# A bidirectional attention and mLSTM layer: a hand-ordered opening with four output tiles, modulation dot products moved later, pauses ahead of TensorE's in-order steps

## The chip, the cores and the metric

The kernel runs on one core of one Trainium2 chip. The metric is the device time of one execution in microseconds (us). Its engines work side by side, each through its own instructions in order: TensorE (PE in the profile, PEld for its weight loads), VectorE (DVE), ScalarE (ACT), GpSimd (POOL), and SyncE (SP), which here only issues DMAs.

## The reference, cut to what matters

One layer over 1024 tokens of width 1024, all in float32:

```python
cond = silu(c)
mod = cond @ w_ada + b_ada                      # 6 x 1024 values: 48 columns of 128
sh1, sc1, g1, sh2, sc2, g2 = split(mod, 6)
h = rms_norm(x, norm_mix_g) * (1 + sc1) + sh1
q_a, k_a, v_a, qk_m, v_m, o_m, gates = split(h @ w_in)
y_attn = axial_gqa_attention(q_a, k_a, v_a)     # 8 heads of 64, 2 key/value heads
y_mem = bidirectional_mlstm(qk_m, v_m, o_m, gates)   # 4 heads of 128, conv of 5 taps before
x = x + g1 * (concat(y_attn, y_mem) @ w_out)
h = rms_norm(x, norm_ffn_g) * (1 + sc2) + sh2
x = x + g2 * ((silu(h @ w_gate) * (h @ w_up)) @ w_down)
return rms_norm(x, final_norm_g)
```

## The kernel before

**Matmuls.** Activations lie transposed: 8 tiles of 128 channels x 1024 tokens. Each float32 product is made of three matmuls on a high and a low part (fp32r): `hi*hi`, `hi*lo`, `lo*hi` (`mm3`, L297 to L300). So each operand is split into a high part by ScalarE (`whi`, `hh`) and a low part by GpSimd or VectorE (`wlo`, `hl`). One output tile of 128 columns takes 2 token halves x 8 channel tiles x 3 = 48 matmuls of 512 columns.

**Order.** The program is one straight list for each engine. It is not written by hand: a planner (`Clock`, `Engine`, `Stream`) keeps a model time, runs chains of steps (`ck.chain`) when their modelled inputs are ready, and lets fill units (`un`) of the list `IN` run on TensorE whenever the main streams would wait by the model. What a step issues on an engine stands in that engine's order for good; if the real time differs from the model's, the engine waits there and all behind it waits too.

**Stages.** (1) The opening (L487 to L611): x is loaded, squares are summed by VectorE and GpSimd into `ssx`, a matmul with `ones` adds over the channels (`ms`, L553), VectorE and ScalarE make 1/rms; warm-up matmuls fill TensorE (`WARM0` 9 and `WARM` 6 calls, L551 and L559). The modulation is a dot product over the condition for each of the 48 columns: a 128 x 1024 tile `ada` of weights, multiplied and summed by one VectorE instruction (`ada_load`, L96 by way of the helper). For each channel tile k two of them (scale and shift) are needed before `h_steps(k)` can make `x*rstd` (VectorE), the scale and shift (ScalarE), `hh` (ScalarE) and `hl` (GpSimd; VectorE for k = 0). TensorE sums three output tiles (the attention's k, v and first q) over k. (2) The rest of the input projection up to the attention, by the list `IN`: the token chunk `t0` with the gate columns, then q tiles, then `f` tiles with their five-tap convolutions; beside it the rotary steps (`rope_steps`) of k and q and the chain of the gates (`gate_steps`), each of which puts small matmuls into TensorE's order (`squares` L641 to L651, `columns` L908, `spread` L922). Meanwhile `ada_late` loads and sums further modulation columns in halves of 512, one for each model microsecond. (3) The attention with fill units. (4) The mLSTM with the last token chunks as fill, then, behind a loop that waits for the last of the 64 late half dot products, the output projection (list `MIX`) as fill. (5) The FFN with its products made by a seven-product scheme; nothing of it is touched.

**Names.** `POOLED` sends the dot product of column 0 to GpSimd and ScalarE. `PP["cond"]` is SiLU(c) on all 128 partitions, loaded 128 times by one DMA of 512 KB. `k2` are the high and low parts of the rotated keys; both must be there before the attention starts. `ready()` ends stage 2: it asks for the last q tile's rotation and the gates.

Of the kernel before, what the change touches and what calls it, by code (L numbers as in the profile page):

```python
# [11 lines left out]
F32 = mybir.dt.float32  # L12
# [3 lines left out]
OP = mybir.AluOpType  # L16
# [24 lines left out]
WARM = 6  # L41
WARM0 = 9
POOLED = (0,)
# [4 lines left out]
IN = ([("t", 0), ("q", 1), ("q", 2), ("q", 3), ("f", 0), ("f", 4), ("f", 1), ("f", 5), ("t", 2), ("f", 2), ("f", 6),  # L48
# [192 lines left out]
def layer_kernel(ctx, tc, xT, c, w_ada, vecs, cons, rope, w_f, w_t0, w_t, w_o, w_gu, w_d, out):  # L241
# [9 lines left out]
    both = const.tile([P, 2], F32, name="both")  # L251
# [6 lines left out]
    nc.scalar.dma_start(con, cons)  # L258
# [30 lines left out]
    nc.vector.tensor_copy(selr, C("sel"))  # L289
    identb = mid.tile([P, P], BF16, name="identb")  # L290
    nc.vector.tensor_copy(identb, ident)
    maskb = mid.tile([P, 2, 2, P], BF16, name="maskb")
    for i in range(2):
        nc.vector.tensor_copy(maskb[:, 0, i], C("maskf"))
        nc.vector.tensor_copy(maskb[:, 1, i], C("maskb"))
# [55 lines left out]
    with tc.manual_schedule():  # L351
# [10 lines left out]
        bp = PP["ada"] = big_open(5)  # L362

# [8 lines left out]
        va = kvp.tile([P, NJ, 2, P], F32R, name="va")  # L372
        k2 = [[kvp.tile([P, S], F32R, name=f"k2{i}{g}") for i in range(2)] for g in range(2)]
# [37 lines left out]
        specs = conv_w(0) + conv_w(1) + conv_w(2)  # L411
# [74 lines left out]
        psum_open("ps0", {n: ("ps0", 8) for n in ("acc", "acct", "ms", "tr", "T")}, 8)  # L486

        def small():
            return stp.tile([P, HALF], F32, tag="sq", name="sq", bufs=4)

        load_cond(bp)
        ck.table = "silu"
        x_t = [stp.tile([P, S], F32, tag="x", name=f"x{k}", bufs=KT) for k in range(KT)]
        msp = [psum_any([P, HALF], "ms") for _ in range(NH)]
        ssx = [stp.tile([P, HALF], F32, tag="ssx", name="ssx", bufs=2) for _ in range(NH)]
        sq_ok = {}
        for k in range(KT):
            def sum_up(k=k):

                for n in range(NH):  # L500
                    sq = ssx[n] if k == 0 else small()
                    act.activation(sq, x_t[k][:, halves(n)], AF.Square)
                    if k:
                        (gps if n and k < 6 else dve).tensor_add(ssx[n], ssx[n], sq)

            sq_ok[k] = ck.chain(dma(x_t[k], xT[k]), sum_up)
        ada_at = {}
        rstd_done = Flag()

        def ada_load(j):  # L510
            t = bp.tile([P, D], F32, tag="big", name="ada")
# [7 lines left out]

        for j in (8, 0):  # L520
            ada_load(j)
        load_piece()
        load_piece()
        ck.need(sq_ok[4])
        load_piece()
# [1561 lines left out]
```

## Time and profile before

| | us |
|---|---|
| median of 3 runs (1403.0 to 1405.35) | 1405.2 |
| the profiled execution | 1407.29 |
| its span, first to last instruction | 1405.5 |
| TensorE busy | 1300.5 (93%) |
| VectorE busy | 1065.1 (76%) |
| ScalarE busy | 662.9 (47%) |
| GpSimd busy | 679.0 (48%) |
| mean granted TensorE clock | 0.972 |

Busy time counts an instruction from start to end; matmuls overlap, so that one of 0.40 us is followed by the next after less. A granted clock of 1.00 is 2.4 GHz and 0.50 is 1.2 GHz. A line of L96 is the helper through which the planner issues all ScalarE, VectorE and GpSimd work: such rows are told apart by their tiles, written out<-in. "[7.23 <-ACT hh L96]" at the end of a row is the idle time of the engine before it and what ended it.

### The profile page before, as it was taken

To read this page: it belongs to the slowest core of one execution; us is meant where nothing else is said; L and a number is where in the kernel's file an instruction comes from. 1 tells how busy PE (TensorE), PEld (TensorE's weight loads), DVE (VectorE), ACT (ScalarE), POOL (GpSimd) and SP (SyncE) were. 2 spreads that over 40 slices of the span, in tenths; PEclk is the share of its full clock that TensorE was granted. 3 is DMA by queue.
4 is the path that set the end of the run, shared out by engine and by line. 5 is a ranking of instruction groups with operands and counts; after the bars stand their busy time and mean duration, and the time that the engine had idled before them with its cause. 6 is when DMAs were issued, how large, how long until landed. Compare 5 with 4: busy or idle time off the path is not lost.

```text
span 1405.5 us, 19481 instructions
## 1 busy us (share of the span) xinstructions
PE 1300.5 (93%) x6594; PEld 1072.1 (76%) x6602; DVE 1065.1 (76%) x1600; ACT 662.9 (47%) x1194; POOL 679.0 (48%) x555
## 2 busy tenths in 40 slices
PE   5789798999999989899996999999999999979997
PEld 2578577889878979777774888888888887757887
DVE  7947979986788848768589886666666654798866
ACT  5454316677666655454476333332332334344463
POOL 5555554545344336577421355454544545545542
PEclk9899989999999999999998999999999999989999
DMA  7446462322122146553552333322332259723324
GB/s 287 165 128 203 135 172 80 108 77 65 38 65 70 35 140 211 188 203 115 196 187 75 113 120 105 107 104 100 110 113 90 71 175 327 275 81 102 93 65 154
DMA packets 103172, 184.40 MB, mean 131 GB/s; under 512 B 11296, under 2 KB 32672, under 8 KB 103072
## 3 DMA queue, kind: packets, MB, share of 16 engines
q1 hardware_dynamic: 89968, 161.06, 36.0%
q10 hardware_dynamic: 13104, 22.10, 4.2%
q8 instruction: 52, 0.85, 0.2%
q14 instruction: 48, 0.39, 0.1%
HBM read 136.19 MB, written 43.25 MB: 128 GB/s over the span
## 4 chain that ended last, share of the span: by engine, by line
PE 61%; DVE 20%; DMA 6%; issue 5%; ACT 3%; POOL 3%; SPq 1%; DVEq 0%; ACTq 0%; POOLq 0%
PE acc L299 15%; PE acc L298 15%; PE acc L300 15%; DVE x L96 3%; PE av L1029 3%; DVE ada L96 3%; DVE sst L96 2%; PE T L1010 2%; DVE PT L96 2%; PE S L978 2%; DVE y L96 1%; PE acct L298 1%; PE acct L300 1%; PE acct L299 1%; DVE wd L96 1%
## 5 line engine op out<-in xcount | busy, mean ns | idle before, releaser
L96 POOL TENSOR_TENSOR wlo<-wst,whi 128x512 fp32r<-128x512 f32 (+2 forms) x196 | 279.5, 1432 | 285.0 <-ACT whi L96 272.9
L96 ACT ACTIVATE whi<-wst 128x512 fp32r<-128x512 f32 (+2 forms) x219 | 131.0, 605 | 125.1 <-POOL wlo L96 25.3
L96 POOL TENSOR_SCALAR P<-P,sst 128x1024 f32<-128x1024 f32 x64 | 88.9, 1392 | 141.1 <-DVE sst L96 106.4
L299 PE MATMUL acc<-x,whi 128*128 128x512 f32 x352 | 140.7, 400 | 5.9 <-DVE x L96 5.9
L96 POOL TENSOR_TENSOR wlo<-wr,whi 128x512 fp32r<-128x512 f32 x56 | 76.9, 1374 | 77.4 <-ACT whi L96 73.9
L298 PE MATMUL acc<-hh,whi 128*128 128x512 f32 x224 | 97.5, 435 | 14.1 <-ACT hh L96 11.8
L298 PE MATMUL acc<-whi,wch 128*128 128x512 f32 x244 | 97.2, 398 | 6.3 <-ACT wch L96 6.3
L96 ACT ACTIVATE P<-S,sst,colq 128x1024 f32<-128x1024 f32 x64 | 77.3, 1207 | 52.4 <-DVE sst L96 47.9
L299 PE MATMUL acc<-hl,whi 128*128 128x512 f32 x224 | 92.4, 412 | 8.2 <-POOL hl L96 4.5
L300 PE MATMUL acc<-whi,wcl 128*128 128x512 f32 x244 | 97.2, 398 | 2.9 <-DVE wcl L96 2.8
L299 PE MATMUL acc<-wlo,wch 128*128 128x512 f32 x244 | 97.0, 398 | 0.6 <-POOL wlo L96 0.5
L96 DVE SCALAR_TENSOR_TENSOR ada<-ada,cond 128x512 f32<-128x512 f32 (+1 forms) x79 | 80.2, 1023 | 18.3 <-DMA ada<-in_w_ada_dram 12.7
L300 PE MATMUL acc<-hh,wlo 128*128 128x512 f32 x224 | 91.5, 409 | 0.0
L96 DVE TENSOR_TENSOR sg<-acc,sg 128x512 f32<-128x512 f32 x67 | 45.4, 687 | 58.8 <-PE acc L300 58.5
L96 ACT ACTIVATE PT<-T 128x512 fp32r<-128x512 f32 x128 | 71.4, 597 | 37.7 <-PE T L1010 36.9
L96 ACT ACTIVATE whi<-wr 128x512 fp32r<-128x512 f32 x60 | 37.9, 632 | 108.1 <-DVE wr L96 50.3
L96 DVE TENSOR_TENSOR PT<-T,PT 128x512 fp32r<-128x512 f32 x128 | 82.8, 681 | 7.2 <-ACT PT L96 7.1
L96 POOL TENSOR_TENSOR wlo<-s,whi 128x512 fp32r<-128x512 f32 x40 | 53.8, 1347 | 70.7 <-ACT whi L96 70.7
L299 PEld LDWEIGHTS acc<-x,whi 128*128 128x128 f32 x352 | 67.0, 190 | 22.3 <-DVE x L96 7.3
L298 PE MATMUL acct<-whi,hh 128*128 128x256 f32 (+1 forms) x256 | 79.4, 310 | 2.5 <-ACT xp L96 1.2
L96 DVE TENSOR_TENSOR wcl<-wd,wch 128x512 fp32r<-128x512 f32 x50 | 48.0, 972 | 42.1 <-ACT wch L96 26.9
L1010 PE MATMUL T<-con,P 128*128 128x128 f32 x512 | 70.3, 275 | 10.2 <-DVE PT L96 7.4
(459 smaller groups left out, 3802.5 us busy)
## 6 DMA issues: line engine op xcount, KB each, us to landing
wr<-in_w_gu_dram SPq DMA_DIRECT2D x66, 256.0 KB, 2.8
ada<-in_w_ada_dram SPq DMA_DIRECT2D x64, 256.0 KB, 3.3
wd<-in_w_d_dram SPq DMA_DIRECT2D x22, 512.0 KB, 7.0
wst<-in_w_gu_dram SPq DMA_DIRECT2D x34, 256.0 KB, 3.1
wst<-act_d SPq DMA_DIRECT2D x33, 256.0 KB, 4.1
ada<-in_w_ada_dram SPq DMA_DIRECT2D x16, 512.0 KB, 5.5
wst<-in_w_o_dram SPq DMA_DIRECT2D x32, 256.0 KB, 4.3
act_d<-sg ACTq DMA_DIRECT2D x31, 256.0 KB, 2.0
```

Of the source, the lines that this page charges most:

```text
L96: return fn(*args, **kw)
L298: nc.tensor.matmul(acc, w[0], x[0], start=first, stop=False)
L299: nc.tensor.matmul(acc, w[0], x[1], start=False, stop=False)
L300: nc.tensor.matmul(acc, w[1], x[0], start=False, stop=last)
L978: nc.tensor.matmul(sp[:, halves(n)], qs[:, j * P:(j + 1) * P], k2[g][m][:, halves(n)], start=m == 0, stop=m == 1)
L1010: nc.tensor.transpose(tp[:, k], Pt[q][:, (4 * b + k) * P:(4 * b + k + 1) * P], ident)
L1029: nc.tensor.matmul(av, va[:, k, h // 4], PT[it][m][:, k], start=(k, m) == (0, 0), stop=(k, m) == (NJ - 1, 1))
```

## The change

- **Opening by hand, four tiles.** The opening's instructions are written out for each engine in a fixed order instead of by the planner (`ve, ac, gp` are the bare engines). TensorE sums four tiles (k, v, first and second q) instead of three, so 24 matmuls for each k, and the list `IN` loses `("q", 1)`. The condition is loaded as one row of 4 KB, SiLU is taken on it, and two matmuls with `ones` spread it over the partitions. The squares are added on VectorE alone (x tiles in pairs), and each pair is summed at once by two matmuls into the same bank. The warm-up is 3 + 3 + 5 calls instead of 9 + 6. `hl` is made by VectorE for every k; `hh` is made by one ScalarE step from x (the separate scaled copy of x is gone); GpSimd makes only the low parts of weights. No dot product goes to GpSimd.
- **Second q tile.** `rope_steps(1)`, which takes its sums out of their banks, is chained behind both halves of `k2`.
- **Dot products later.** No late half dot product is issued in stage 2; the attention takes 32 (before: up to 48 by its end); the other 32 are issued beside the whole mLSTM, first in the old pool, then in another four-buffer ring once the first tiles of the attention's output are split. The loop that waits for the last of them stands behind the mLSTM instead of ahead of the output projection.
- **Pauses.** `later(dt)` adds model time: 2.5 us ahead of `squares`, 6.0 us ahead of the `columns` transposes, 5.0 us ahead of `spread`.

```diff
-WARM = 6
-WARM0 = 9
-POOLED = (0,)
+WARM = 5
+WARM0 = 3
+NT0 = 4
-IN = ([("t", 0), ("q", 1), ("q", 2), ("q", 3), ("f", 0), ("f", 4), ("f", 1), ("f", 5), ("t", 2), ("f", 2), ("f", 6),
+IN = ([("t", 0), ("q", 2), ("q", 3), ("f", 0), ("f", 4), ("f", 1), ("f", 5), ("t", 2), ("f", 2), ("f", 6),
...
+        gp.memset(crow, 0.0)
+        nc.sync.dma_start(crow[0:1], c)
+        for k in range(KT):
+            nc.sync.dma_start(x_t[k], xT[k])
...
+        ac.activation(both[:, 2:3], eps, AF.Silu)
+        ac.activation(crow[0:1], crow[0:1], AF.Silu)
+        ac.activation(both[:, 2:3], eps, AF.Abs_reciprocal_sqrt)
+        for n in range(NH):
+            nc.tensor.matmul(cb[n], ones, crow[:, halves(n)], start=True, stop=True)
...
+            if k % 2:
+                for n in range(NH):
+                    nc.tensor.matmul(msp[n], ones, a[:, halves(n)], start=k == 1, stop=k == KT - 1)
+                if k < KT - 1:
+                    nc.tensor.matmul(acc0[0][0], ones, crow[:, 0:HALF], start=True, stop=True)
...
+        dot(8)
+        gain(0)
+        root_v(0)
+        root_y(0)
+        ac.activation(msp[0], ry[0], AF.Square)
+        first_hi(0, 0)
+        first_lo(0, 0, gp)
+        dot(0)
+        shift(0)
+        root_y(1)
+        root_end(0)
+        first_hi(0, 1)
+        first_lo(0, 1, gp)
+        xr(0, 0)
+        h_hi_of(0, 0)
+        root_v(1)
...
+        def prepare(k):
+            if k + 1 < KT:
+                if k > 1:
+                    ada_load(9 + k)
+                ada_load(k + 1)
+            dot(8 + k)
+            gain(k)
+            dot(k)
+            shift(k)
             for n in range(NH):
+                xr(k, n)
+                h_hi_of(k, n)
+            for n in range(NH):
+                h_lo_of(k, n)
+            if k < 5:
+                first_hi(1, k - 1)
+                first_lo(1, k - 1, gp)
...
-            ck.chain(0.0, lambda: evac(0), lambda: evac(1), swap, squares)
+            ck.chain(0.0, lambda: evac(0), lambda: evac(1), swap, later(2.5), squares)
...
-                     lambda: exps(0), lambda: exps(1), state, lambda: exps(2),
+                     lambda: exps(0), lambda: exps(1), state, lambda: exps(2), later(6.0),
...
+                     lambda: dve.tensor_scalar(cols[:, :, 1], cols[:, :, 1], QK, None, op0=OP.mult), decay, later(5.0), spread,
...
+        rope_steps(4, [(a, Flag()) for a in acc0[0]])
         v_steps([(a, Flag()) for a in acc0[1]])
-        rope_steps(4, [(a, Flag()) for a in acc0[0]])
         ck.at(2.5, lambda: rope_steps(0, [(a, Flag()) for a in acc0[2]]))
+        ck.chain(0.0, *k2_ok, lambda: rope_steps(1, [(a, Flag()) for a in acc0[3]]))
...
         def ready():
-            if ck.t > t_ada[0]:
-                ada_late()
-                t_ada[0] = ck.t + 1.0
...
-        while len(adas) < 48:
+        while len(adas) < 32:
...
-        while not summed:
-            ck.need(*adas[-2:])
-            ada_late(64)
-        ck.tick = None
+        ck.need(*adas[-2:])
+        PP["ada_new"] = lambda: mp.tile([P, HALF], F32, tag="yat", name="ada", bufs=4)
+        ck.tick = lambda: (0, 0) in Y and all(y[2].done for y in Y[0, 0]) and ada_late(64)
...
         ck.streams([un], stop=lambda: not open_sum[0])
+        while not summed:
+            ck.need(*adas[-2:])
+            ada_late(64)
+        ck.tick = None
```

## Rows read from the trace of the kernel before

**Rows 1.** The table by stage: for each stretch (us from the span's start) its length, then busy us and instructions of each engine, granted clock, busy share of the DMA engines, GB/s. The stretches are the opening, the rest of the projection ahead of the attention, the attention, the mLSTM with the last token chunks, and the mLSTM with the output projection.

```profile
0.00:89.00 89.00, 58.26 (x179) 36.65 (x180) 66.12 (x96) 45.77 (x71) 48.00 (x34) 0.88 0.58 205
89.00:206.00 117.00, 104.30 (x546) 88.25 (x545) 92.84 (x139) 42.42 (x68) 60.46 (x37) 0.93 0.55 164
206.00:506.00 300.00, 284.92 (x1871) 249.57 (x1869) 254.21 (x428) 196.78 (x343) 133.48 (x99) 1.00 0.23 67
506.00:582.00 76.00, 66.51 (x466) 61.92 (x470) 52.04 (x135) 37.80 (x101) 38.97 (x59) 0.96 0.58 180
582.00:700.00 118.00, 111.63 (x543) 89.28 (x546) 82.51 (x156) 58.06 (x137) 83.80 (x98) 1.00 0.58 194
```

**Rows 2.** The timeline of TensorE in the opening: start us, us, engine, line, instruction, and in brackets the idle time before it.

```profile
22.72 1.12 PE L553 MATMUL ms<-ssx,ones 128*128 128x512 f32 x2 [1.63 <-DVE ssx L96]
...
36.23 0.79 PE L298 MATMUL acc<-hh,whi 128*128 128x512 f32 x1 [7.23 <-ACT hh L96]
40.75 0.79 PE L299 MATMUL acc<-hl,whi 128*128 128x512 f32 x1 [3.73 <-DVE hl L96]
...
49.65 0.39 PE L299 MATMUL acc<-hl,whi 128*128 128x512 f32 x1
49.88 0.40 PE L300 MATMUL acc<-hh,wlo 128*128 128x512 f32 x1
...
88.75 0.40 PE L300 MATMUL acc<-hh,wlo 128*128 128x512 f32 x1
```

**Rows 3.** The timeline of TensorE's weight loads under the warm-up calls (two loads for each call).

```profile
7.90 0.50 PEld L551 LDWEIGHTS acc<-con,ones 128*128 128x128 f32 x2 [7.90 <-issue]
...
13.19 0.34 PEld L551 LDWEIGHTS acc<-con,ones 128*128 128x128 f32 x1 [0.52 <-issue]
14.03 0.19 PEld L551 LDWEIGHTS acc<-con,ones 128*128 128x128 f32 x1 [0.51 <-issue]
14.46 0.19 PEld L551 LDWEIGHTS acc<-con,ones 128*128 128x128 f32 x1 [0.24 <-issue]
```

**Rows 4.** The timeline of ScalarE at the start: the table load, SiLU of the condition, and one scale and shift of half a tile.

```profile
1.64 1.28 ACT L96 ACT_TABLE_LOAD   x1 [1.64 <-PEq L2075]
5.71 1.06 ACT L96 ACTIVATE cond<-cond 128x1024 f32<-128x1024 f32 x1 [2.79 <-DMA cond<-in_c_dram]
...
58.12 0.82 ACT L96 ACTIVATE x<-x,mod,sc 128x512 f32<-128x512 f32 x1 [2.80 <-DVE x L96]
```

**Rows 5.** The timeline of VectorE over one period of two channel tiles of the opening (57.40 to 69.38).

```profile
57.40 0.69 DVE L96 TENSOR_TENSOR x<-x,sq 128x512 f32<-128x512 f32 x1
58.01 1.22 DVE L96 SCALAR_TENSOR_TENSOR ada<-ada,cond 128x1024 f32<-128x1024 f32 x1
...
59.15 0.69 DVE L96 TENSOR_TENSOR x<-x,sq 128x512 f32<-128x512 f32 x1
...
61.80 2.29 DVE L96 SCALAR_TENSOR_TENSOR ada<-ada,cond 128x1024 f32<-128x1024 f32 x1
...
64.01 1.77 DVE L96 TENSOR_TENSOR x<-x,sq 128x512 f32<-128x512 f32 x1
...
69.38 0.69 DVE L96 TENSOR_TENSOR x<-x,sq 128x512 f32<-128x512 f32 x1
```

**Rows 6.** The timeline of GpSimd in the same period, and its low parts of the keys `k2` after the opening.

```profile
61.43 1.57 POOL L96 TENSOR_TENSOR hl<-x,hh 128x512 fp32r<-128x512 f32 x1 [0.44 <-ACT hh L96]
63.46 1.77 POOL L96 TENSOR_TENSOR hl<-x,hh 128x512 fp32r<-128x512 f32 x1 [0.46 <-ACT hh L96]
...
119.16 5.22 POOL L96 TENSOR_TENSOR k<-kdup,k 128x1024 fp32r<-128x1024 f32 x2 [9.99 <-ACT k L96]
```

**Rows 7.** Whom TensorE waited for from 89 to 206 us: us in total, times, the longest.

```profile
PE T L922 <- DVE dexp L96: 4.7, 1, 4.7
PE T L908 <- ACT T L96: 4.2, 2, 3.1
PE ms L651 <- ACT sqk L96: 2.3, 2, 1.8
```

**Rows 8.** The timeline of TensorE behind two of these waits: the first matmuls, and those at which the time of one falls again.

```profile
138.53 0.63 PE L299 MATMUL acc<-hl,whi 128*128 128x512 f32 x1
...
143.65 0.44 PE L299 MATMUL acc<-hl,whi 128*128 128x512 f32 x1
...
179.96 0.63 PE L299 MATMUL acc<-hl,whi 128*128 128x512 f32 x1
...
184.65 0.42 PE L298 MATMUL acc<-hh,whi 128*128 128x512 f32 x1
```

**Rows 9.** The table by stretch for the instructions on the tiles `ada` alone: length, then busy us and instructions of VectorE, ScalarE, GpSimd, granted clock, DMA share, GB/s (two VectorE instructions for each dot product).

```profile
89.00:206.00 117.00, 28.30 (x60) 0.00 (x0) 0.00 (x0) 0.93 0.55 164
206.00:300.00 94.00, 17.25 (x36) 0.00 (x0) 0.00 (x0) 1.00 0.35 104
506.00:560.00 54.00, 12.85 (x32) 0.00 (x0) 0.00 (x0) 1.00 0.70 217
```

**Rows 10.** The view of the tile `ada` from 506 to 600 us: for how long VectorE stood still ahead of a dot product until its weights had landed (us, times).

```profile
  DMA ada<-in_w_ada_dram: 6.0, 2
```

**Rows 11.** Whom TensorE waited for from 506 to 700 us (us, times, the longest): the first line.

```profile
PE ni L1814 <- DVE num L96: 6.9, 4, 4.3
```

**Rows 12.** The table by stretch, columns as in rows 1, for ten microseconds of the output projection's start.

```profile
590.00:600.00 10.00, 9.49 (x46) 7.07 (x45) 7.76 (x13) 5.05 (x14) 8.16 (x13) 1.00 1.06 378
```

More of the change, by code (lines that the diff above doesn't have):

```diff
@@ L486, in layer_kernel @@
         psum_open("ps0", {n: ("ps0", 8) for n in ("acc", "acct", "ms", "tr", "T")}, 8)
+        ve, ac, gp = nc.vector, nc.scalar, nc.gpsimd
         def small():
             return stp.tile([P, HALF], F32, tag="sq", name="sq", bufs=4)
[L491 to L511, printed above, removed]
[L512 to L532 removed]
         def rstd_steps(ms, scale, tag, put, flag=None):
@@ new lines, in first_load @@
+        def first_load(b, f):
+            i = 4 * b + f
+            wst_t[b, f] = (wp.tile([P, 4, P], F32, tag="wst", name="wst", bufs=3) if i < 3 else room[i - 3])
+            nc.sync.dma_start(wst_t[b, f], w_f[f][:, 4 * b:4 * b + 4])
+        for j in (8, 0):
+            ada_load(j)
+        for f in range(NT0):
+            first_load(0, f)
+        for j in (9, 1, 10):
+            ada_load(j)
+        nc.sync.dma_start(con, cons)
+        for f in range(NT0):
+            first_load(1, f)
@@ new lines, in layer_kernel, with first_hi, first_lo @@
+        W0 = {}
+        def first_hi(b, f):
+            if (b, f) in ((1, 2), (1, 3)):
+                i = 2 * (f - 2)
+                if not i:
+                    W0["more"] = kvp.tile([P, 4, 4, P], F32R, tag="va", name="more")
+                W0[b, f] = [W0["more"][:, i + j] for j in range(2)]
+            else:
+                W0[b, f] = [wp.tile([P, 4, P], F32R, tag="w" + t, name="w" + t) for t in ("hi", "lo")]
+            ac.activation(W0[b, f][0], wst_t[b, f], AF.Copy)
+        def first_lo(b, f, eng):
+            eng.tensor_sub(W0[b, f][1], wst_t[b, f], W0[b, f][0].bitcast(F32))
@@ new lines, in mm @@
+        def mm(k, f, n, i):
+            w, h = W0[k // 4, f], (h_hi[k][:, halves(n)], h_lo[k][:, halves(n)])
+            a, b = ((0, 0), (0, 1), (1, 0))[i]
+            nc.tensor.matmul(acc0[f][n], w[a][:, k % 4], h[b], start=(k, i) == (0, 0), stop=(k, i) == (KT - 1, 2))
+        acc0 += [[psum_any([P, HALF], "acc") for _ in range(NH)] for _ in range(2)]
+        ck.until(24.0)
+        for k in range(KT):
+            if k + 1 < KT:
+                prepare(k + 1)
+            seq = [(f, n, i) for n in range(NH) for f in range(NT0) for i in range(3)]
+            if k == 0:
+                seq = [(f, n, i) for n in range(NH) for i in range(3) for f in range(NT0)]
+            elif k == KT - 1:
+                seq = [(f, n, i) for f in range(NT0) for n in range(NH) for i in range(3)]
+            for f, n, i in seq:
+                mm(k, f, n, i)
+                ck.pe(0.23)
+                if n == 1 and i == 2 and (k == 3 or k == 7 and f < 2):
+                    load_piece()
@@ L618, in layer_kernel, with later, wait @@
         rp = []
+        def later(dt):
+            def wait():
+                ck.fin = ck.now + dt
+            return wait
         def rope_steps(i, accs):
```

161 lines of the change are left out of this document (80 added, 81 removed).

## The prediction

> **What bounds the kernel now.** I read the table by stage first, because the change touches four stages and a share of the whole span says nothing about one of them. TensorE is busy 285 of 300 us in the attention and 112 of 118 us beside the output projection, but only 58 of 89 us in the opening, and 104 of the next 117 [rows 1]. So beyond 206 us TensorE sets the pace, and what can be won lies ahead of it. The second view is TensorE's timeline in the opening. The sum of squares is out at 22.72 + 1.12 = 23.8 us; the first matmul of the projection starts at 36.23, the second, held by a low part `hl`, at 40.75, and the last of the three tiles' 144 ends at 88.75 + 0.40 = 89.15 [rows 2]. At full clock one follows the other after 49.88 - 49.65 = 0.234 us [rows 2], so 144 need 33.7 us: the opening costs 55 us that are no product. The third view, VectorE over two channel tiles, says who paces it: from 57.40 to 69.38, 5.99 us for each tile, without a gap [rows 5].
>
> **Prices on VectorE.** A dot product of 1024 takes 59.15 - 58.01 = 1.14 us alone, an operation on half a tile 58.01 - 57.40 = 0.61 [rows 5]. Beside GpSimd the same two take 64.01 - 61.80 = 2.21 and about 1.70 [rows 5], while GpSimd makes `hl` at 61.43 and 63.46 [rows 6]: each GpSimd operation on half a tile adds 1.1 us to VectorE, once.
>
> **The opening, step by step.** *Sum of squares.* The condition's row is 4 KB instead of 512 KB, and its SiLU (1.06 us, start 5.71 [rows 4]) should end by 5.1 to 6.8 us, though GpSimd's memset and a second table load (1.28 [rows 4]) are ahead of the squares. TensorE then has 16 float32 calls in order (2 for the condition, 3 + 3 for warmth, 8 for the squares) before 1/rms can start. A call is two passes: 2 x 0.85 us at the lower clock (1.2 GHz), 2 x 0.43 at the higher (2.4 GHz), which came 6.1 us after the first call [rows 3]. So 3.6 calls in 6.1 us, 12.4 at 0.86, together 16.8 us: squares out at 22 to 23.6 us. I take 22, only 1.8 us earlier than now. ScalarE's squares (1024 at the 1.06 us of the SiLU [rows 4]) are done by 16 and do not bind.
>
> *First tile.* VectorE's order from 21 us (the first half's sum) is: root 0.6, dot 1.14, two root steps 1.2, `xr` 0.66, root 0.6, `hl` 0.66, two root steps 1.2, `xr` 0.66, a wait for ScalarE's `hh` of 0.82 [rows 4], `hl` 0.66: 8.8 with small ones. The four weight parts on GpSimd add 4 x 1.1. That is 34 us (0.66 is an estimate: the 0.61 of rows 5 and a pointer operand). Some high parts are there at 27 to 28, so TensorE starts some 8 us earlier than at 36.23. The five warm-up calls end about 26; should the clock fall in the gap, its price (0.43 instead of 0.234 for the first dozen, below) is hidden, since VectorE is what TensorE waits for.
>
> *Steady state.* For each further k VectorE has two dots 2.28, four half-tile operations 2.64, two small ones 0.25, and some 0.3 waiting for `hh`: 5.5; GpSimd adds 1.1 for k = 1 to 4 (first weights), and about as much for k = 5 to 7 (four pieces of `t0`): 6.6. TensorE needs 24 x 0.234 = 5.6, so VectorE still binds. Seven times 6.6 from 34: 80. Then the last tile's remaining 21 matmuls: **the four tiles end at 85 us.** Before, the same four end at 89.15 + 48 x 0.234 = 100.4. **Gain 15.** Bounds: GpSimd adds nothing and the roots come at 20: 76, gain 24; each GpSimd operation (1.57 to 1.77 us long [rows 6]) hits two VectorE operations: 94, gain 6. The loads (16 x 512 KB of `ada`, five buffers, on SP in order) lead VectorE by two tiles, more than 11 us, so SP's waits for a free buffer hide.
>
> GpSimd's price is where a rule of the Trainium skill bears on the sum. The rows put it at 1.1 us for each operation [rows 5, 6]. GPSIMD Engine Reference, section 8, says that GpSimd shares its SBUF interfaces with VectorE and contends with VectorE instructions that have two SBUF inputs; by that rule, the trace agrees, and the change is on the wrong side of it where it puts nearly all two-input work of the opening on VectorE and leaves twelve low parts of weights beside it. By the rows the sum is 1381, by the rule taken at its hardest 1388 (a rival below).
>
> **From the opening to the attention.** The waits of TensorE here that pauses answer to are 4.7 (`spread`), 4.2 (`columns`) and 2.3 us (`squares`) [rows 7]. Behind two of them the clock is at its lower level: from 138.53 to 143.65 twelve matmuls take 0.427 each, from 179.96 to 184.65 eleven [rows 8], together 23 x 0.193 = 4.4 us lost, and about 3 more in the small matmuls ahead of them. So 18.6 us. The pauses put 2.5, 6.0 and 5.0 us of other matmuls ahead of these steps. Queued behind a waiting step is all of TensorE's order; the fill that covers the pause is q and `f` tiles, which have to be done anyway. The longest waits are 1.8, 3.1 and 4.7 [rows 7], so two are covered amply and the third by 0.3; but the 30 late dot products (60 instructions, 28.3 us of VectorE [rows 9]) leave the stretch as well, which brings the gate chain forward. Against it: the gates are ready later in the planner, one more conv unit gets ahead of the attention, and its taps come among the chain. **I take 12 of 18.6**; bounds 0 (the lag moves with the step) and 19.
>
> **Attention.** 32 dots instead of the 18 that fell into it (36 instructions [rows 9]): 14 more of about 0.7 us, 10 us on VectorE, in a stage where TensorE idles 15 of 300 us and VectorE 46 [rows 1]. Cost 0 to 4, taken 2. The conv unit that went ahead (11 us) is missing as fill here or at the end of the mLSTM: cost 0 to 6, taken 2.
>
> **mLSTM.** At its end of the token chunks TensorE stands 4.3 us for `num` [rows 11] and lower clock follows; the waiting loop for the last dots sits near it and moves behind. Gain 0 to 6, taken 3. Sixteen more dots: 11 us on VectorE, busy 82.5 of 118 [rows 1], and 16 x 256 KB more on DMA engines that are full at 590 to 600 [rows 12]. Cost 0 to 8 short of the rival below, taken 2. The FFN starts earlier and is as before: its modulation sums come in behind the mLSTM, still ahead of it.
>
> **The sum.** -15 - 12 + 2 + 2 - 3 + 2 = -24. The profiled execution took 1407.3 us (span 1405.5), 2.1 above the median, so 1383 for such an execution and **1381 for the median.**
>
> **The rivals.**
> *More is won:* opening near its good bound (20) and stalls gone whole (18), the rest even: 1367. For it: VectorE's order has no wait by chance any more, and the late dots are out of the gate chain.
> *GpSimd costs its whole length:* VectorE's denser list meets each of the twelve GpSimd operations for all of its 1.57 to 1.77 us [rows 6] instead of 1.1: 0.6 more each, 7 us: 1388. The period of rows 5 speaks against it: there VectorE had no gap either, and paid 1.1. The skill's rule above would have it so.
> *The pauses win nothing net:* the step comes later but its inputs too, or the fill spent ahead of the attention is missing at the mLSTM's end; or they are without effect because the planner's clock is not the chip's. Opening 12, rest zero: 1393. For it: the last wait's margin is 0.3 us. Against it: the planner lost to real lags by a few us only.
> *Banks held:* the second q tile keeps two of eight banks until both halves of `k2` are done. In the trace that is 119.16 + 5.22 = 124.4 [rows 6], 35 us behind the opening's end. If the sums of `t0` come to need these two banks after some 8 us, TensorE stands up to 27 us in order, less what the missing dots bring `k2` forward, say 15: 1396. Against it: six banks can carry sums of 3 us each.
> *Slower:* the late dots on VectorE wait for their weights in its order, ahead of `num`, `W` and `Cs` on which the mLSTM's matmuls wait. Now two such waits cost 6.0 us, 3.0 each [rows 10], while the DMA engines were 0.70 busy [rows 9]; the sixteen new ones stand where they are full [rows 12]. At 3.0 us each VectorE loses 48, and with some 30 of it reaching TensorE (which already waits for `num` [rows 11]): 1411. It decides once landing regularly exceeds what the planner reckons; below that VectorE's slack (35 us of 118 [rows 1]) hides it.
>
> **How the numbers follow.** Forecast 0.52; more 0.15; GpSimd's whole length 0.05; nothing from pauses 0.11; banks 0.08; slower 0.09. A measurement of this kernel tells a difference from none at about 0.2% (3 us). All but the last are faster by more, 0.91 together; 0.04 of it I move to within 0.2%, for pauses and banks going wrong at once with the opening's bad bound (1381 + 12 + 9 = 1402): faster 0.87, within 0.04, slower 0.09. The range leaves out the slower case and the outer part of the best: 1362 to 1398, which takes in the opening's bounds (gain 24: 1372; gain 6: 1390) and the pauses' (1374 and 1393).
>
> **What would show it.** In the changed kernel: squares out at 22 us; projection matmuls from about 28 and dense from 34; VectorE without gaps at 6.6 us for each k, and the fourth tile done at 85 (76 to 94); no wait of over 1 us at `squares`, `columns` and `spread`, the clock at 1.00 through the stretch; first scores of the attention some 20 us earlier than now, with one conv unit more behind it; no VectorE waits for `ada` weights in the mLSTM. I am wrong if TensorE waits for a bank under `t0`, if a dot product ahead of `num` waits for its load, or if the gain of the first 200 us is given back between the attention and the FFN.

## The result, and the profile after

The changed kernel takes 1409.39 us (median of 18 runs, 1404.95 to 1413.08) against 1405.46 (18 runs, 1402.68 to 1407.94): a ratio of 1.0029 [1.002, 1.0039], so slower by 0.29%. The profiled execution has a span of 1408.2 us, 2.7 above that of before, and the same mean clock, 0.972.

**The opening did what was forecast.** TensorE's timeline of the changed kernel (start, us, instruction; columns as in [rows 2]):

```profile
19.52 0.59 PE L587 MATMUL ms<-sqw,ones 128*128 128x512 f32 x1
...
26.26 0.73 PE L668 MATMUL acc<-hh,whi 128*128 128x512 f32 x2 [1.86 <-ACT hh L612]
...
33.63 1.09 PE L668 MATMUL acc<-hh,wlo 128*128 128x512 f32 x4
...
84.98 0.39 PE L668 MATMUL acc<-hh,more 128*128 128x512 f32 x1
```

The last sum of squares is out at 20.1 us, the first product starts at 26.26, and the fourth tile ends at 85.4, where before it would have been 100.4. VectorE paces it, as this period of its timeline shows:

```profile
51.30 2.31 DVE L546 SCALAR_TENSOR_TENSOR ada<-ada,cond 128x1024 f32<-128x1024 f32 x1
...
53.79 1.22 DVE L546 SCALAR_TENSOR_TENSOR ada<-ada,cond 128x1024 f32<-128x1024 f32 x1
...
55.13 1.40 DVE L609 SCALAR_TENSOR_TENSOR x<-x,sc,sq 128x512 f32<-128x512 f32 x2
56.66 1.42 DVE L615 SCALAR_TENSOR_TENSOR hl<-x,mod,hh 128x512 fp32r<-128x512 f32 x2
57.99 2.32 DVE L546 SCALAR_TENSOR_TENSOR ada<-ada,cond 128x1024 f32<-128x1024 f32 x1
```

One k takes 57.99 - 51.30 = 6.69 us, and the first of two equal dot products takes 2.31 instead of 1.22, as in [rows 5] beside a GpSimd operation, here this one:

```profile
51.19 1.34 POOL L543 TENSOR_TENSOR more<-spare,more 128x512 fp32r<-128x512 f32 x1 [5.36 <-DMA wst<-in_w_t_dram]
```

**Where the lead went.** The table by stage, cut at the first scores and at the last matmuls of the attention (tile `av`) and of the mLSTM (`ni`). First the kernel after, then the mLSTM's row of the kernel before (its other boundaries: first scores 205.6, last `av` 503.8). Columns as in [rows 1]:

```profile
0.00:85.00 85.00, 72.20 (x234) 47.00 (x235) 65.91 (x101) 36.94 (x56) 23.12 (x20) 0.94 0.59 209
85.00:194.50 109.50, 100.06 (x546) 85.57 (x545) 75.51 (x87) 41.92 (x66) 55.23 (x38) 0.95 0.45 122
194.50:502.10 307.60, 291.97 (x1965) 258.70 (x1964) 256.57 (x448) 196.75 (x347) 131.97 (x98) 1.00 0.25 77
502.10:661.80 159.70, 138.27 (x749) 114.55 (x748) 124.83 (x292) 75.82 (x200) 104.44 (x138) 0.95 0.60 199
```

```profile
503.80:656.80 153.00, 139.49 (x852) 121.49 (x859) 109.68 (x257) 78.18 (x207) 97.69 (x137) 0.98 0.59 190
```

The scores start 11.1 us earlier, the attention ends 1.7 earlier, the mLSTM ends 5.0 later. In the mLSTM TensorE has 103 instructions less, and VectorE 15 us of work more. Times alone mislead, though, since fill may be done earlier or later. So I count TensorE's **lead** over the kernel before at a boundary: the time by which it comes earlier, plus the fill matmuls done more by then (0.234 us for one of 512 columns [rows 2], and half of that, an estimate, for one of 256). At the first scores one unit of 48 is done more: 11.1 + 11.2 = 22.3 us. At the attention's end it is 20.0 (156 more matmuls of 256 columns), **at the mLSTM's end 5.5** (45 more of 512 columns, 5.0 us later), and at the FFN's first sum of squares -3.5. From there to the end 673.3 us against 674.1: the FFN is as before. So the lead is lost in the mLSTM and right behind it.

A lead is read from one execution of each kernel. The changed kernel and e6, e12, e17 and e18 below are the same program up to the attention's end: their scores start at 193.3 to 194.9 us, their attention ends at 501.7 to 502.5. Up to there a lead can be read to some 2 us; over the whole span single executions spread more (e10's profiled one is 5.7 us under its median, e2's 2.9).

### The profile page after: what moved, and what is told of

It is laid out like the page before. It is cut to its first block, busy times and chain, and to the rows that moved or that the text cites. A ratio compares the mean times of both kernels' runs of the same rounds, so it can differ in the third digit from the quotient of the medians.

```text
span 1408.2 us, 19440 instructions
## 1 busy us (share of the span) xinstructions
PE 1310.2 (93%) x6610; PEld 1077.5 (77%) x6610; DVE 1064.0 (76%) x1605; ACT 649.4 (46%) x1173; POOL 645.7 (46%) x536
## 4 chain that ended last, share of the span: by engine, by line
PE 53%; DVE 28%; issue 6%; DMA 5%; ACT 4%; POOL 2%; SPq 1%; DVEq 0%; ACTq 0%; POOLq 0%
PE acc L293 13%; PE acc L292 13%; PE acc L294 13%; DVE sst L96 4%; DVE y L96 3%; DVE PT L96 3%; DVE x L96 2%; PE av L1118 2%; DVE ada L96 2%; PE T L1099 2%; PE S L1067 2%; DMA v<-v_d 1%; DVE ada L546 1%; PE acct L292 1%; PE acct L293 1%
## 5 line engine op out<-in xcount | busy, mean ns | idle before, releaser
L96 POOL TENSOR_TENSOR wlo<-wst,whi 128x512 fp32r<-128x512 f32 (+2 forms) x188 | 267.7, 1430 | 287.4 <-ACT whi L96 280.4
L96 ACT ACTIVATE whi<-wst 128x512 fp32r<-128x512 f32 (+2 forms) x211 | 126.1, 605 | 118.6 <-PE acc L294 25.4
L96 ACT ACTIVATE PT<-T 128x512 fp32r<-128x512 f32 x128 | 72.4, 596 | 45.4 <-PE T L1099 44.8
L293 PEld LDWEIGHTS acc<-x,whi 128*128 128x128 f32 x352 | 66.9, 190 | 22.3 <-DVE x L96 7.3
L1099 PE MATMUL T<-con,P 128*128 128x128 f32 x512 | 71.8, 275 | 10.2 <-DVE PT L96 9.0
L96 DVE TENSOR_REDUCE sst<-S 128x1 f32<-128x1024 f32 x64 | 77.6, 1213 | 4.6 <-PE S L1067 4.6
L1099 PEld LDWEIGHTS T<-con,P 128*128 128x128 f32 x512 | 57.4, 140 | 21.7 <-issue 10.8
L293 PE MATMUL acct<-wlo,hh 128*128 128x256 f32 (+1 forms) x256 | 72.5, 283 | 0.0
L294 PE MATMUL acct<-whi,hl 128*128 128x256 f32 (+1 forms) x256 | 72.4, 283 | 0.0
```

Of the source, the lines that this page charges most:

```text
L96: return fn(*args, **kw)
L293: nc.tensor.matmul(acc, w[0], x[1], start=False, stop=False)
L294: nc.tensor.matmul(acc, w[1], x[0], start=False, stop=last)
L1099: nc.tensor.transpose(tp[:, k], Pt[q][:, (4 * b + k) * P:(4 * b + k + 1) * P], ident)
```

## The experiments

All in one table; us from the profiled execution, ratio and interval against the kernel before. "Length" is from the first scores to the last `av`, from there to the last `ni`, and from there to the FFN's first sum. Half dots are the half dot products issued in the attention and beside the mLSTM. e6, e11, e17 and e18 leave part of the modulation out: they price the dots and are no kernels to use.

| run | half dots | first scores | lengths | lead at scores, attention's end, mLSTM's end | median us | ratio |
|---|---|---|---|---|---|---|
| before | 18, 16 | 205.6 | 298.2, 153.0, 74.6 | 0, 0, 0 | 1405.5 | |
| after | 32, 32 | 194.5 | 307.6, 159.7, 73.1 | 22.3, 20.0, 5.5 | 1409.4 | 1.0029 [1.002, 1.0039] |
| e1 opening | 24, 16 | 196.0 | 310.5, 159.1, 77.3 | 14.5, 11.3, -3.9 | 1420.7 | 1.0107 [1.0089, 1.0126] |
| e2 pauses | 19, 16 | 202.1 | 298.9, 149.8, 73.4 | 3.5, 2.8, 6.0 | 1402.4 | 0.9978 [0.9962, 0.9993] |
| e3 dots | 32, 32 | 196.0 | 306.6, 169.4, 73.2 | 9.6, 4.0, -11.0 | 1420.7 | 1.0108 [1.009, 1.0126] |
| e4 opening, pauses | 21, 16 | 209.0 | 308.0, 166.0, 71.8 | 7.8, 2.2, -16.4 | 1429.9 | 1.0182 [1.016, 1.0204] |
| e7 opening, dots | 32, 32 | 187.6 | 305.8, 166.4, 72.9 | 18.0, 13.2, 1.2 | 1408.3 | 1.0013 [1.0, 1.0026] |
| e8 pauses, dots | 32, 32 | 191.1 | 305.9, 168.5, 73.7 | 14.5, 9.6, -4.5 | 1412.7 | 1.0042 [1.0026, 1.0058] |
| e5 hold t3 | 32, 32 | 194.0 | 310.3, 155.8, 73.3 | 22.8, 7.9, 1.6 | 1408.4 | 1.0017 [1.0005, 1.0029] |
| e9 hold all t | 32, 32 | 192.0 | 324.3, 200.4, 40.1 | 24.8, -49.0, -54.3 | 1465.3 | 1.0411 [1.039, 1.0431] |
| e6 none in mLSTM | 32, 0 | 193.3 | 308.9, 144.3, 72.1 | 23.5, 19.9, 20.8 | 1395.9 | 0.9917 [0.9895, 0.994] |
| e11 none in attention | 0, 32 | 195.1 | 301.3, 160.5, 73.4 | 21.7, 24.2, 10.4 | 1403.1 | 0.9964 [0.9951, 0.9977] |
| e12 condition's wait | 32, 32 | 194.9 | 307.3, 161.8, 73.4 | 21.9, 19.9, 3.3 | 1410.0 | 1.002 [1.0007, 1.0032] |
| e17 loads only | 32, 0 | 193.3 | 308.4, 147.5, 72.7 | 23.5, 20.4, 18.1 | 1398.1 | 0.9932 [0.9918, 0.9947] |
| e18 no loads | 32, 32 | 193.8 | 308.7, 160.5, 72.9 | 23.0, 19.6, 4.3 | 1410.4 | 1.0018 [1.0005, 1.0031] |
| e10 all in attention | 64, 0 | 194.8 | 315.0, 141.5, 72.4 | 22.0, 16.5, 16.0 | 1402.7 | 0.9964 [0.9948, 0.9979] |
| e13 the same, no pauses | 64, 0 | 187.6 | 311.4, 151.2, 76.0 | 18.0, 11.8, 15.0 | 1399.3 | 0.9956 [0.9944, 0.9969] |
| e14 e13 with old opening | 64, 0 | 198.8 | 314.4, 152.0, 74.0 | 6.8, -2.4, 0.0 | 1411.3 | 1.003 [1.0017, 1.0044] |
| e15 before, 34 in attention | 34, 0 | 207.0 | 312.7, 138.2, 78.8 | -1.4, -10.3, -7.4 | 1408.6 | 1.0031 [1.0015, 1.0047] |
| e16 e15 with new opening | 40, 0 | 198.4 | 314.7, 143.4, 72.8 | 12.1, 7.5, 10.8 | 1404.0 | 0.9983 [0.9972, 0.9993] |

My theory at first was that the lead turns into fill done early, because TensorE sets the attention's pace and the plan puts the fill there; the rivals were that pauses or moved dots eat it.

### The parts one by one and in pairs (e1 to e4, e7, e8)

Each keeps or undoes whole parts of the diff; the pauses and the placing of the dots are these lines:

```diff
-            ck.chain(0.0, lambda: evac(0), lambda: evac(1), swap, squares)
+            ck.chain(0.0, lambda: evac(0), lambda: evac(1), swap, later(2.5), squares)
...
-        def ada_late(last=48, ahead=2):
+        def ada_late(last=32, ahead=2):
...
-            if ck.t > t_ada[0]:
-                ada_late()
-                t_ada[0] = ck.t + 1.0
```

> The changed kernel's opening, its list IN and the second q tile behind k2, but the late dot products where they stood before and no pauses. Theory (a lead of TensorE ahead of the attention turns into fill that is done early, and the attention and the mLSTM keep their own length): fourth tile at 85 us as in the changed kernel, the last token chunk tens of us earlier than 581.6, TensorE idler and at a lower clock in the mLSTM, the time 1400 to 1407, so at most a third of the 15 us shows. Rival (the moved dots and the pauses are what eats the gain): the 15 us show almost whole, 1389 to 1394.

> The kernel before with the three pauses and nothing else. Theory (lead turns into fill): the waits at columns and spread shrink, the first scores come within 4 us of before, the time 1402 to 1408. Rival (the pauses bring the gates later in the plan, and what is put ahead is missing as fill later): 1409 to 1415. Forecast on record for this part: a gain of 12, 1393.

> The kernel before with the late dot products moved (none ahead of the attention, 32 in it, 32 beside the mLSTM) and nothing else. Theory in its plain form (only the fill decides): 1404 to 1409. Rival (the 14 more dots in the attention and the 16 more in the mLSTM lengthen these two stages, because VectorE sets their pace there): attention and mLSTM together 8 to 16 us longer, the time 1409 to 1418, though the stage ahead of the attention, without its 30 dots, gets up to 8 us shorter.

> The changed kernel with the late dot products back where they stood before: new opening and pauses. If the moved dots are what eats the gain: 1383 to 1392. If the lead turns into fill done early: 1400 to 1408, with the mLSTM as idle on TensorE as in the changed kernel.

> The changed kernel without the three pauses. If the pauses pay as they do alone (first scores 3.5 us earlier, 0.2%): 1411 to 1416. If they cost with this opening, as the opening with pauses is slower than the opening alone: 1395 to 1405.

> The kernel before with the pauses and the moved dot products, without the new opening. If the parts add up (dots +14, pauses -3): 1415 to 1419, first scores at 193 to 196 us. If the opening's lead is what feeds on the moved loop, and pauses and dots hinder each other: 1420 to 1426.

Only e2 came as the theory had it; e7 (1408.3) and e8 (1412.7) lie outside both of their readings. **e1 and e4** are slower than either reading gave: the opening alone costs 1.07%. The stretches of e1 in which it happens, columns as in [rows 1], VectorE in the middle of them, and whom TensorE and VectorE waited for from 535 to 562 us:

```profile
530.00:540.00 10.00, 6.34 (x38) 4.97 (x36) 6.99 (x15) 3.33 (x9) 8.65 (x15) 0.99 0.88 287
540.00:550.00 10.00, 2.77 (x9) 2.02 (x9) 5.43 (x15) 2.60 (x8) 4.15 (x5) 0.50 0.56 184
550.00:560.00 10.00, 5.43 (x17) 4.69 (x18) 3.46 (x12) 0.39 (x1) 0.00 (x0) 0.50 0.64 199
```

```profile
547.20 0.69 DVE L96 SCALAR_TENSOR_TENSOR ada<-ada,cond 128x512 f32<-128x512 f32 x1 [0.96 <-DMA ada<-in_w_ada_dram]
547.82 0.08 DVE L96 DVE_READ_ACCUMULATOR ada<-ada,cond 128x1 f32 x1
548.91 0.69 DVE L96 SCALAR_TENSOR_TENSOR ada<-ada,cond 128x512 f32<-128x512 f32 x1 [1.01 <-DMA ada<-in_w_ada_dram]
```

```profile
PE ni L1901 <- DVE num L96: 11.1, 2, 9.2
DVE ada L96 <- DMA ada<-in_w_ada_dram: 6.8, 6, 2.0
```

The token chunks end at 535 instead of 582 us, and so the loop for the last dots, which in the kernel before stands ahead of the output projection, is reached when those dots are not yet loaded. From 540 to 554 VectorE does hardly anything but dots, nearly each behind its load, and `num`, on which TensorE waits 9.2 us at a clock of 0.50, is queued behind them. This is the rival called slower in the prediction, in the old place of the dots and with the new opening. With the dots and their loop moved, VectorE waits 2.4 us for these loads in the whole mLSTM of e7, and with the new opening the move gains 0.9% (e1 to e7) and 1.5% (e4 to after). How much of that is the loop and how much the other places of the dots was not separated.

**e3** shows what the same move costs by itself: 1.08%. The first scores come 9.6 us earlier, for the 30 half dots that left the stage ahead; the attention gets 8.4 and the mLSTM 16.4 us longer, more than the 8 to 16 expected.

**The pauses** (e2 against before, e8 against e3, after against e7, e4 against e1) bring -0.2, -0.7, +0.2 and +0.7%: nothing on the whole. By TensorE's lead at the first scores they gain 3.5, 4.9 and 4.3 us in the first three pairs and cost 6.7 in the last, where `spread` waits 10.7 us in e4 in spite of its pause (0.8 in e1). Whom TensorE waited for between opening and scores, in the changed kernel and in e7, the same without pauses:

```profile
PE ms L737 <- ACT sqk L96: 5.9, 1, 5.9
PE acc L292 <- ACT xp L96: 3.6, 2, 2.8
```

```profile
PE T L1008 <- DVE dexp L96: 5.4, 1, 5.4
PE T L994 <- ACT T L96: 3.1, 2, 2.4
PE ms L737 <- ACT sqk L96: 1.8, 1, 1.8
```

The waits at `spread` and `columns` (8.5 us) are gone, but a whole unit of 48 matmuls, 11.2 us, is put in ahead of the attention, and `squares` waits 5.9 us instead of 1.8. The scores come 6.9 us later with the pauses than without, with 11.2 us of fill more behind them.

### Is it the fill? (e5, e9)

Fill is held back until the attention's own streams have ended: in e5 the last token chunk, in e9 the last three, moved behind the convolution units.

```diff
             for kind, i in order:
+                if (kind, i) in [('t', 3)]:
+                    yield [att_done]
```

> The changed kernel with the last token chunk held back until the attention's own streams have ended, so that some 84 matmuls of fill move from the attention into the mLSTM. Theory (TensorE sets the attention's pace, fill put into it lengthens it, and the mLSTM then lacks it): each of these costs between (307.6 - 298.2) / 108 = 0.09 us (the attention's growth over the fill matmuls it got more) and 0.234 us, so the attention gets 7 to 18 us shorter, the mLSTM keeps its 150 to 160 us with less idle time on TensorE, and the time is 1391 to 1402. Rival (VectorE's 14 more dot products set the attention's length): the attention stays at 304 us or more, TensorE idles in it, and the time is 1405 to 1415.

> The changed kernel with the token chunks t2, t1 and t3 all behind the convolution units and held back until the attention's streams have ended: 468 matmuls of 272 columns (468 x 0.124 us by their share of a 512-column matmul's 0.234, so 58 us) leave the attention. If TensorE sets the attention's pace, as its 15 idle us of 308 say: the attention gets 40 to 58 us shorter (250 to 268). If the attention has a length of its own, through VectorE and ScalarE, and the fill only lies in its gaps, as in the run that held back t3: 298 to 312, TensorE idle for over 50 us of it, and the time 1430 to 1460.

Both go against my theory. In e5 10 us of fill leave the attention and it gets 2.7 us longer. In e9 55 us of fill leave it (468 matmuls, of 256 columns by the trace), and its second half has none at all; the two halves, columns as in [rows 1], and whom TensorE waits for in the second:

```profile
192.00:367.00 175.00, 154.23 (x860) 128.94 (x858) 162.37 (x277) 103.35 (x176) 75.49 (x56) 0.94 0.33 99
367.00:516.00 149.00, 112.51 (x637) 96.21 (x637) 94.34 (x173) 84.86 (x146) 41.99 (x34) 0.85 0.06 15
```

```profile
PE T L1099 <- DVE PT L96: 37.2, 24, 2.6
```

TensorE is idle for 36 of 149 us, the view of waits puts it down to `PT` of VectorE, which is itself busy for 94 of the 149, and the attention takes 324 us, not 250 to 268, and more than the 298 to 312 of the other reading too. The lower clock doesn't explain it: at a clock of 1.00 TensorE's busy time would be shorter by 0.06 x 154 + 0.15 x 112.5 = 26 us at most (an estimate from the two rows), and 298 is left, for 55 us of fill taken out. So the attention has a length of its own, in its second half with no engine full, and most of the fill lies in its gaps: that TensorE is 95% busy there doesn't make it the bound.

### Is it the dots, and where? (e6, e11, e12)

e6 leaves out the 32 half dots beside the mLSTM, e11 the 32 in the attention, e12 only asks for the first one later:

```diff
-        ck.tick = lambda: ada_late(64)
+        t_cond = ck.t + 14.0
+        ck.tick = lambda: ck.t > t_cond and ada_late(64)
```

> The changed kernel without the 32 half dot products beside the mLSTM and without their loads (modulation columns 32 to 47 then hold only their bias: this part of the computation is left out). Theory that the dots lengthen the mLSTM through VectorE: from the attention's end to the mLSTM's end 148 to 154 us instead of 159.7, the time 1399 to 1404. Rival (the mLSTM lacks fill, its clock falls, and VectorE's dots lie in its waits): 157 us or more, 1406 to 1410.

> The changed kernel without the 32 late half dot products in the attention and without their loads (modulation columns 16 to 31 then hold only their bias: this part of the computation is left out). If the dots lengthen the attention through VectorE: attention 285 to 296 instead of 307.6. If the attention's length comes from the fill: 305 to 310.

> The changed kernel with the first dot product beside the mLSTM 14 us of the plan's time later, so that VectorE no longer stands 9.3 us ahead of it for the condition (loaded again and put through SiLU at the mLSTM's start). If that wait holds up the mLSTM's chain, which is queued behind it on VectorE: mLSTM 4 to 9 us shorter, the time 1400 to 1406. If VectorE had nothing to do in it: 1407 to 1412, the dots only come later.

e6 settles where the lead is lost. The mLSTM's row, as in the first table by stage:

```profile
502.20:646.50 144.30, 129.73 (x749) 109.09 (x749) 97.72 (x225) 76.13 (x200) 94.63 (x138) 1.00 0.51 162
```

With the same fill (749 instructions of TensorE in both) the mLSTM is 15.4 us shorter, more than expected, and the lead goes through it whole: 19.9 to 20.8. So it isn't fill that the mLSTM lacked. Of the 15.4 us, 6.9 are less idle time of TensorE (14.6 for 21.4), and 8.5 are the same matmuls taking less time (129.73 busy for 138.27) at a granted clock of 1.00 instead of 0.95: by these rows more than half of what the dots cost there comes through TensorE's clock. GpSimd, too, takes 9.8 us less for the same 138 instructions. e11 says that 32 half dots in the attention cost 6.3 us, less than the 11.6 to 22.6 expected from them: 0.2 us each, against 0.48 beside the mLSTM. e12 finds VectorE's wait for the condition to be without effect. Two lines of VectorE's waits in the changed kernel's mLSTM, and the first line of e12's:

```profile
DVE ada L96 <- ACT cond L96: 9.3, 1, 9.3
...
DVE ada L96 <- DMA ada<-in_w_ada_dram: 0.9, 1, 0.9
```

```profile
DVE W L96 <- DMA o_d<-vstg: 14.5, 1, 14.5
```

Where the 9.3 us are gone, VectorE stands 14.5 us ahead of `W` instead: it would have stood in that time anyway.

### VectorE's time or the loads? (e17, e18)

e17 keeps the loads, their order and their waits and takes away the dots' time; e18 keeps the time and takes away the loads (first block e17, second e18, ahead of the line that issues a half dot):

```diff
+            if n >= 32:
+                adas.append(ck.chain(dma(t, w_ada[j][:, halves(i)]),
+                                     lambda: dve.tensor_copy(modacc[:, i, j:j + 1], t[:, 0:1])))
+                return
...
+            if n >= 32:
+                cnd = PP["cond"][:, halves(i)]
+                adas.append(ck.chain(4.0, lambda: dve.scalar_tensor_tensor(
+                    t, cnd, 1.0, cnd, op0=OP.mult, op1=OP.mult, accum_out=modacc[:, i, j:j + 1])))
+                return
```

> The changed kernel in which each of the 32 half dot products beside the mLSTM is replaced by a copy of one column of its weights: all loads and the waits for them stay, VectorE's 0.6 us and more for each are gone (the modulation columns 32 to 47 are not computed: this part of the computation is left out). If VectorE's time is the price: mLSTM 143 to 149 us instead of 159.7, the time 1395 to 1400, as without the dots. If the loads are (DMA engines shared with the weights of the output projection, landing waits in VectorE's order): 156 to 162, 1406 to 1411.

> The changed kernel in which the 32 half dot products beside the mLSTM are taken of the condition with itself, without loading their weights (the modulation columns 32 to 47 are not computed: this part of the computation is left out); each comes 4 us of the plan after it is asked for, in place of the load's time. If VectorE's time is the price: mLSTM 154 to 164, the time 1404 to 1411. If the loads are: 143 to 149, 1395 to 1400.

Both came as the theory of VectorE's time has it. The mLSTM's rows of e17 and e18:

```profile
501.70:649.20 147.50, 134.02 (x749) 112.45 (x747) 96.73 (x260) 75.02 (x200) 95.81 (x138) 0.97 0.65 216
```

```profile
502.50:663.00 160.50, 137.15 (x749) 111.65 (x748) 120.85 (x292) 75.39 (x200) 104.88 (x138) 0.96 0.45 146
```

With the loads, and with 24 to 28 us less work on VectorE than in e18 and the changed kernel, most of the lead stays (20.4 to 18.1). Without the loads, but with VectorE's work, it is lost (19.6 to 4.3), as in the changed kernel. GpSimd goes with VectorE's work, not with the loads (95.81 us in e17, 104.88 in e18), so part of the price may lie in what the dots do to GpSimd; the runs don't separate that. In the changed kernel VectorE is not full over the whole mLSTM (124.83 of 159.70), but it is 93% busy in 30 us in which TensorE idles for 6.5 (columns as in [rows 1]):

```profile
620.00:630.00 10.00, 8.25 (x48) 6.90 (x47) 9.56 (x23) 5.19 (x15) 7.30 (x9) 1.00 0.25 82
630.00:640.00 10.00, 7.81 (x46) 6.33 (x45) 9.04 (x22) 3.94 (x12) 7.82 (x12) 1.00 0.24 67
640.00:650.00 10.00, 7.40 (x33) 5.43 (x32) 9.42 (x17) 4.25 (x11) 9.47 (x11) 0.96 0.23 79
```

### All late dots in the attention (e10, e13 to e16)

In all five no dot is issued beside the mLSTM, and the condition is not loaded again for them (e12 finds that load without effect); e10 has the rest of the change, e13 leaves out the pauses, e14 the new opening too; e15 and e16 also keep the half dots ahead of the attention (30 and 24).

```diff
-        def ada_late(last=32, ahead=2):
+        def ada_late(last=64, ahead=2):
...
-        while len(adas) < 32:
+        while len(adas) < 64:
...
-        ck.tick = lambda: ada_late(64)
```

> The changed kernel with all 64 late half dot products in the attention and none beside the mLSTM. If the dots beside the mLSTM cost 13.5 us (as the run without them says) and the attention's second half has VectorE to spare (33 of 155 us idle): mLSTM 144 to 148 us, attention 308 to 313, the time 1396 to 1403. If each dot in the attention costs what the 14 added ones seem to (9.4 us, 0.67 each): attention 320 to 329, the time 1408 to 1417.

> The changed kernel without pauses and with all 64 late half dot products in the attention. If the time follows the first scores (187.6 us without pauses against 194.5 with them): attention 308 to 314 us, mLSTM 141 to 147, the time 3 to 7 us below the run with pauses (1402.7), 1395 to 1400. If it follows TensorE's lead (one unit of 48 matmuls, 11 us, is left for later without the pauses): the mLSTM takes up the 7 us, 1401 to 1406.

> The kernel before with all 64 late half dot products in the attention, none ahead of it and none beside the mLSTM; old opening, no pauses. If the time follows the first scores (196.0 in the run that only moved the dots, 194.8 in the changed kernel with all dots in the attention): within 4 us of that kernel's 1402.7. If the opening's 15 us of TensorE count once the mLSTM has no dots: 1409 to 1418.

> The kernel before with its 30 late half dots ahead of the attention as they are, and the other 34 in the attention, none beside the mLSTM. By the prices so far (0.2 us for a half dot in the attention, 0.5 beside the mLSTM): first scores at 205 us, attention 298 + 16 x 0.2 = 301, mLSTM 153 - 16 x 0.5 = 145, the time 1399 to 1402. If dots cost the same wherever they stand: 1404 to 1408.

> The new opening, no pauses, the late half dots ahead of the attention as in the kernel before, and all others in the attention. If the 15 us of the stall in the run of the opening alone (its loop for the last dots) are all that hid the opening: 1395 to 1401, below the same with the old opening by 4 or more. If the attention's and the mLSTM's own lengths hide it: within 3 us of the same with the old opening.

e10 and e13 beat both kernels, at ratios of 0.9964 and 0.9956, the lowest of the kernels that compute everything; their intervals overlap with each other and with e2's. e13's time lies where the first reading put it, but its mLSTM is 9.7 us longer than e10's, with 829 instructions of TensorE for 709, which is the second reading: what the scores gained by doing less fill is paid when that fill is done in the mLSTM. e13 against e14 says what the opening is worth once the mLSTM has no dots: 0.9956 / 1.003, 0.74% or 10 us of its 15. e16 against e15 gives 0.48%, some 7 us, though e16 itself stays above the 1395 to 1401 expected. e15 came as its rival had it (1408.6 for 1404 to 1408). Its mLSTM is 14.8 us shorter than before, but 11.9 of these are fill that is done elsewhere, so that 16 half dots fewer give 2.9 us of lead; its attention is 14.5 longer instead of 3, of which 5.6 are fill, so that 16 more cost 8.9 of lead. A half dot's price is therefore no constant. In the attention it is 0.2 us of length (0.1 to 0.15 of lead) from e11 to after to e10, and 0.9 (0.56 of lead) from before to e15. In the mLSTM the 16 of the kernel before cost 2.9 us of lead, and the 32 of the changed kernel 15.3 (e6). I have no run that settles why; the plan places fill and dots anew in each kernel.

## Why the prediction failed

By its own steps, in us of TensorE's lead:

| step | predicted | measured |
|---|---|---|
| opening | 15 | 100.4 - 85.4 = 15.0 |
| to the first scores | 12 | 22.3 - 15.0 = 7.3 |
| attention (2 + 2) | -4 | 20.0 - 22.3 = -2.3 |
| mLSTM (3 - 2) | 1 | 5.5 - 20.0 = -14.5 |
| to the FFN's sum | 0 | -3.5 - 5.5 = -9.0 |
| FFN | 0 | 0.8 |
| sum | 24 | -2.7 |

- **Opening:** right in size and in mechanism. VectorE took 6.69 us for each k for a forecast 6.6, and the end came at 85.4 for 85. The marks ahead of it were some 2 us off, without effect on the end: squares out at 20.1 for 22, products from 26 for 28, and dense from 36.6 for 34. The price of GpSimd beside VectorE held: 2.31 - 1.22 = 1.09 us for an operation of 1.34, so not its whole length.
- **Ahead of the attention:** 7.3 for 12. I had given the 12 to the pauses and named the dots that left only as a help. By the runs the parts don't add up: the dots that left bring 9.6 us of lead by themselves (e3) and 3.5 with the new opening (e1 to e7), the pauses on top of both 4.3 (e7 to after), and without the dots moved they cost 6.7 (e1 to e4). In the time, though, the pauses won nothing (after against e7, +0.2%), and there the rival "pauses win nothing net" was right: the step comes later, and the fill ahead of it is more. One unit more ahead of the attention was forecast; no wait of over 1 us at `squares`, a clock of 1.00 and scores 20 us earlier were not met (5.9, 0.95, 11).
- **Attention:** right in size, which was partly luck: the reason behind it, that TensorE sets the pace there, is wrong (below).
- **mLSTM: the step that failed.** For sixteen more half dots I set VectorE's 35 idle us of 118 [rows 1] against 11 more us of dots ([rows 9] would have given 12.85) and took a cost of 2. Both sides were wrong. VectorE's time for the dots went from 12.85 us in the kernel before to 32.31, 19.5 more. And idle time of VectorE is no measure of what it can take on, since VectorE is on the mLSTM's chain: 32 half dots beside it cost 15.4 us of length (e6), more than half of VectorE's 27 us for them, partly as waits of TensorE and partly as a lower clock; and it goes with VectorE's work, not with the loads (e17, e18). In the kernels with 32 half dots there the lead falls by 12.0 to 16.6 us in the mLSTM (e3, e7, e8, e11, e12, e18, after; 6.3 and 5.3 in e5 and e9, which hold fill back for it), in those with none it changes by -0.5 to 3.3, and by -2.3 in e17 with the loads alone. The gain of 3 for the moved loop was not to be had: in the kernel before it cost nothing, in e1 the new opening would have made it cost a stall.
- **Behind the mLSTM:** put at nothing, without a reason. 45 matmuls of the output projection (10.5 us) were done early, yet the stretch to the FFN took 73.1 us for 74.6. TensorE waits there for the mLSTM's last results, split into `yah`; first the changed kernel from 661 to 735 us, then the same line of the kernel before from 657 to 731:

```profile
PE acc L292 <- ACT yah L96: 6.4, 1, 6.4
```

```profile
PE acc L298 <- ACT yah L96: 0.6, 1, 0.6
```

  So of 10.5 us that were held as such fill, 1.5 came out as time. e6 and e10 lose about 8 in the same place, with 6.5 and 6.7 us for `yah`: so this loss does not come from the dots beside the mLSTM.
- **The first claim**, that TensorE sets the pace beyond 206 us, was read from busy shares of 95% [rows 1] and is wrong for the attention: e5 and e9 took fill out of it, and it got no shorter.
- **The slower rival** had the right stage and nearly the time (1411), by luck: its mechanism is not the one at work. VectorE waited 0.9 us for the dots' loads in the changed kernel's mLSTM, not 48, and without the loads (e18) the lead is lost all the same. Its mechanism is real, but in e1. *Banks held* did not show: no such wait is among the rows. One of the prediction's own signs of being wrong came true: what was gained by the first scores is given back between the attention and the FFN.

Open is why the attention's length differs between plans beyond what the dots explain (310.5 with 24 in e1, 306.6 with 32 in e3, 312.7 with 34 in e15).

## What to carry over

A share of 95% on an engine that is fed with fill can say how well gaps are filled, and not that the engine is the bound: take fill away and see whether the stage gets shorter. Move side work by its price per stage, measured by leaving it out there (in the changed kernel, on the mean, 0.2 us for a half dot in the attention, 0.48 beside the mLSTM), not by the idle time of its engine, and measure it again in another plan: it was no constant here. Gains ahead of a stage count only if each later stage can pass them on, so follow a lead boundary by boundary, fill included.

## What was not expected of the hardware

The 32 half dots beside the mLSTM take 32.31 us of VectorE, 1.01 each (view of the tile `ada`):

```profile
502.10:661.80 159.70, 32.31 (x64) 0.95 0.60 199
```

In e1's stall, where GpSimd has little to do, one takes 0.69, with its accumulator read 0.69 + 0.08. The one among them that takes 1.45 meets a GpSimd operation:

```profile
544.79 1.45 DVE L96 SCALAR_TENSOR_TENSOR ada<-ada,cond 128x512 f32<-128x512 f32 x1 [0.22 <-DMA ada<-in_w_ada_dram]
```

```profile
543.91 1.77 POOL L96 TENSOR_TENSOR wlo<-wst,whi 128x512 fp32r<-128x512 f32 x1 [3.94 <-ACT whi L96]
```

Beside the mLSTM GpSimd is busy for 104 of the 160 us. The Trainium skill's GPSIMD Engine Reference, section 8, says that GpSimd contends with VectorE's two-input instructions for SBUF. By that rule, the trace agrees: 1.45 for 0.69 beside a GpSimd operation, 1.01 for 0.77 on the mean beside the mLSTM. That this is all of the difference on the mean is not shown.
